# Loops over one ring of rows in place of written-out programs, and two tiny transfers ahead of the others, in a LoRA matrix product on one core

## The chip, the cores and the metric

The kernel runs on one core of a Trainium2 chip. The core has five engines with programs of their own: PE (TensorE, matrix products), DVE (VectorE), ACT (ScalarE), POOL (GpSimd) and SP (SyncE, which here only issues transfers). They meet through semaphores. Transfers between the device's memory and the core's SBUF are issued by SP or ACT and carried by 16 DMA engines, among which each transfer is divided. The metric is the device time of one execution in microseconds (us); lower is better.

## The reference

```python
def reference(x, W, lora_A, lora_B, lora_E, scale):
    x_flat = x.reshape(-1, in_dim)          # 32768 x 256, float32
    y = x_flat @ W                          # W: 256 x 256
    lora_out = x_flat @ lora_A              # 256 x 16
    lora_out = lora_out * lora_E
    lora_out = lora_out @ lora_B            # 16 x 256
    y = y + scale * lora_out
    return y.reshape(batch, seq_len, out_dim)
```

x has 16 x 2048 rows of 256 values, 33.55 MB; the output is as large. Both pass through the core once.

## The kernel before

The rank-16 part is folded into the weights first: weff = W + scale * A diag(E) B, so that each row of x needs one product with a 256 x 256 matrix. PE transposes lora_A (L194), DVE scales it (L132), PE multiplies it by lora_B (L198), DVE adds W (L138, weff in bf16).

The 32768 rows are cut into nine tiles by PLAN (L10): 16 row groups, seven times 32, and 16 again, where a row group is one row for each of the 128 partitions. A 32-row tile is 4096 KB. Each tile is loaded into one of six buffers xy0 to xy5 (SLOTS) of 32 row groups, in which a partition holds 32 consecutive rows, and the result is written over x in the same buffer and stored from there.

SP issues all of the large transfers, in an order that is written out by hand: W (L104), the loads of tiles 0 to 5 (LEAD, L102), and then for each tile a wait until ACT has reported it ready (s_rdy) and its store (L109). After the store of tile 2 come the loads of tiles 6, 7 and 8 (AFTER); each waits until the store that frees its buffer has landed (s_out). All of these use one queue, SP's, so they are carried in this order. ACT issues the three small loads of lora_A, lora_B and lora_E on its own queue (L158 to L160).

The computing runs in 64 steps of four row groups (Q = 4). In a step DVE casts 128 x 1024 values of x to bf16 (xb, L146); PE transposes them in eight blocks into PSUM (ps_xt, L176); DVE copies the transposed blocks to SBUF (xt, L155); PE multiplies them by weff in eight matmuls into PSUM (ps_y, L184); ACT copies the result into the x buffer (L163). xb, xt, ps_xt and ps_y exist twice and alternate. After the last step of a tile, ACT drains and raises s_rdy (L165).

The programs of DVE and ACT are written out: 64 steps one after the other, with waits on rising counts (s_t, s_p). Only PE's program is a loop, of 31 turns with two steps each (L202); there a wait takes its count back down (take, L169). DVE casts one step ahead, and PE transposes one step ahead: the order on PE is transposes of step k + 1, products of step k. DVE itself waits for each tile's load (s_in).

POOL makes the identity matrix for the transposes (L118, L120) and has nothing else to do.

Of the kernel before, what the change touches and what calls it, by code (L numbers as in the profile page):

```python
# [6 lines left out]

PLAN = [16] + [32] * 7 + [16]  # L10

ROWS, SLOTS = 32, 6

LEAD = 6
AFTER = {2: [6, 7, 8]}

Q = 4


@with_exitstack  # L20
def kernel(
    ctx: ExitStack,
    tc: tile.TileContext,
    x: bass.AP,
    W: bass.AP,
    lora_A: bass.AP,
    lora_B: bass.AP,
    lora_E: bass.AP,
    scale: bass.AP,
    out: bass.AP,  # L30
):
    nc = tc.nc
    P = 128
    FP32 = mybir.dt.float32
    BF16 = mybir.dt.bfloat16

    x_flat = x.flatten_outer_dims()
    out_flat = out.flatten_outer_dims()
    N, K = x_flat.shape
    M = out_flat.shape[1]  # L40
    R = lora_B.shape[0]
    KC = K // P
    CHUNKS = len(PLAN)
    assert K == M and sum(PLAN) * P == N and all(b % Q == 0 for b in PLAN)

    def sbuf(name, shape, dt):
        return ctx.enter_context(nc.sbuf_tensor(name, shape, dt))

    def psum(name, shape, dt):
        return ctx.enter_context(nc.psum_tensor(name, shape, dt))  # L50

    xy = [sbuf(f"xy{s}", [P, ROWS, K], FP32) for s in range(SLOTS)]
    xb = [sbuf(f"xb{s}", [P, Q, K], BF16) for s in range(2)]
    xt = [sbuf(f"xt{s}", [P, Q, KC, P], BF16) for s in range(2)]
    w_sb = sbuf("w_sb", [P, KC, M], FP32)
    a_sb = sbuf("a_sb", [P, KC, R], FP32)
    b_sb = sbuf("b_sb", [R, M], FP32)
    e_sb = sbuf("e_sb", [R, 1], FP32)
    b_bf = sbuf("b_bf", [R, M], BF16)
    ate = sbuf("ate", [R, KC, P], BF16)  # L60
    weff = sbuf("weff", [P, KC, M], BF16)
    ident = sbuf("ident", [P, P], FP32)
    ident_bf = sbuf("ident_bf", [P, P], BF16)

    ps_xt = [psum(f"ps_xt{s}", [P, Q, KC, P], BF16) for s in range(2)]
    ps_y = [psum(f"ps_y{s}", [P, Q, M], FP32) for s in range(2)]
    ps_at = psum("ps_at", [P, KC, P], FP32)
    ps_aeb = psum("ps_aeb", [P, KC, M], FP32)

    sem = tc.alloc_semaphore  # L70
    s_w, s_a, s_b, s_e = sem("s_w"), sem("s_a"), sem("s_b"), sem("s_e")
    s_in = [sem(f"s_in{i}") for i in range(CHUNKS)]

    again = CHUNKS - SLOTS
    s_out = [sem(f"s_out{i}") for i in range(again + 1)]
    s_id = sem("s_id")
    s_lora = sem("s_lora")
    s_lpe = sem("s_lpe")
    s_xb = sem("s_xb")
    s_t = sem("s_t")  # L80
    s_xt = sem("s_xt")
    s_p = sem("s_p")
    s_y = sem("s_y")
    s_rdy = sem("s_rdy")

    starts = [sum(PLAN[:i]) * P for i in range(CHUNKS)]

    def rows_of(flat, i):
        b, r0 = PLAN[i], starts[i]
        return flat[r0:r0 + b * P, :].rearrange("(p b) k -> p b k", b=b)  # L90


    steps = [(i, r) for i, b in enumerate(PLAN) for r in range(0, b, Q)]
    n = len(steps)
    assert n % 2 == 0

    with tc.tile_critical(sync_engine=mybir.EngineType.SP, no_gpsimd_drain=True):  # L97
        sp, pe, dve, act, pool = nc.sync, nc.tensor, nc.vector, nc.scalar, nc.gpsimd


        def load(i):
            sp.dma_start(out=xy[i % SLOTS][:, :PLAN[i], :], in_=rows_of(x_flat, i)).then_inc(s_in[i], 16)  # L102

        sp.dma_start(out=w_sb[:], in_=W.rearrange("(c p) m -> p c m", p=P)).then_inc(s_w, 16)  # L104
        for i in range(LEAD):
            load(i)
        for i in range(CHUNKS):
            sp.wait_ge(s_rdy, i + 1)
            sp.dma_start(out=rows_of(out_flat, i), in_=xy[i % SLOTS][:, :PLAN[i], :]).then_inc(s_out[min(i, again)], 16)  # L109
            for later in AFTER.get(i, []):  # L110
                if later >= SLOTS:
                    sp.wait_ge(s_out[later - SLOTS], 16)
                load(later)
        for i in range(len(s_out) - 1):
            sp.wait_ge(s_out[i], 16)


        pool.memset(ident[:], 0.0).then_inc(s_id, 1)  # L118
        pool.wait_ge(s_id, 1)
        pool.affine_select(  # L120
            out=ident[:], in_=ident[:], compare_op=mybir.AluOpType.not_equal, fill=1.0,
            base=0, pattern=[[-1, P]], channel_multiplier=1,
        ).then_inc(s_id, 1)


        dve.wait_ge(s_id, 2)
        dve.tensor_copy(out=ident_bf[:], in_=ident[:]).then_inc(s_lora, 1)  # L127
        dve.wait_ge(s_b, 16)
        dve.tensor_copy(out=b_bf[:], in_=b_sb[:]).then_inc(s_lora, 1)  # L129
        dve.wait_ge(s_e, 16)  # L130
        dve.wait_ge(s_lpe, 1)
        dve.tensor_scalar(  # L132
            out=ate[:], in0=ps_at[:R, :, :], scalar1=e_sb[:], scalar2=float(scale),
            op0=mybir.AluOpType.mult, op1=mybir.AluOpType.mult,
        ).then_inc(s_lora, 1)
        dve.wait_ge(s_w, 16)
        dve.wait_ge(s_lpe, 2)
        dve.tensor_add(out=weff[:], in0=w_sb[:], in1=ps_aeb[:]).then_inc(s_lora, 1)  # L138

        def round_step(k):  # L140
            i, r = steps[k]
            if r == 0:
                dve.wait_ge(s_in[i], 16)
            if k >= 2:
                dve.wait_ge(s_t, k - 1)
            dve.tensor_copy(out=xb[k % 2][:], in_=xy[i % SLOTS][:, r:r + Q, :]).then_inc(s_xb, 1)  # L146

        round_step(0)
        for k in range(n):
            if k + 1 < n:  # L150
                round_step(k + 1)
            dve.wait_ge(s_t, k + 1)
            if k >= 2:
                dve.wait_ge(s_p, k - 1)
            dve.tensor_copy(out=xt[k % 2][:], in_=ps_xt[k % 2][:]).then_inc(s_xt, 1)  # L155


        act.dma_start(out=a_sb[:], in_=lora_A.rearrange("(c p) r -> p c r", p=P)).then_inc(s_a, 16)  # L158
        act.dma_start(out=b_sb[:], in_=lora_B).then_inc(s_b, 16)
        act.dma_start(out=e_sb[:], in_=lora_E[:, None]).then_inc(s_e, 16)  # L160
        for k, (i, r) in enumerate(steps):
            act.wait_ge(s_p, k + 1)
            act.copy(out=xy[i % SLOTS][:, r:r + Q, :], in_=ps_y[k % 2][:]).then_inc(s_y, 1)  # L163
            if r + Q == PLAN[i]:
                act.drain().then_inc(s_rdy, 1)  # L165

        def take(s):  # L169
            pe.wait_ge(s, 1).then_inc(s, -1)  # L170

        def transposes(k):
            take(s_xb)
            for j in range(Q):
                for c in range(KC):
                    t = pe.transpose(ps_xt[k % 2][:, j, c, :], xb[k % 2][:, j, c * P:(c + 1) * P], ident_bf[:])  # L176
            t.then_inc(s_t, 1)

        def products(k):
            take(s_xt)  # L180
            take(s_y)
            for j in range(Q):
                for c in range(KC):
                    m = pe.matmul(  # L184
                        ps_y[k % 2][:, j, :], xt[k % 2][:, j, c, :], weff[:, c, :],
                        start=(c == 0), stop=(c == KC - 1),
                    )
            m.then_inc(s_p, 1)

        pe.sem_inc(s_y, 2)  # L190
        pe.wait_ge(s_a, 16)
        pe.wait_ge(s_id, 2)
        for c in range(KC):
            t = pe.transpose(ps_at[:R, c, :], a_sb[:, c, :], ident[:])  # L194
        t.then_inc(s_lpe, 1)
        pe.wait_ge(s_lora, 3)
        for c in range(KC):
            m = pe.matmul(ps_aeb[:, c, :], ate[:, c, :], b_bf[:], start=True, stop=True)  # L198
        m.then_inc(s_lpe, 1)
        transposes(0)  # L200
        pe.wait_ge(s_lora, 4)
        with pe.Fori(0, n // 2 - 1):  # L202
            transposes(1)
            products(0)
            transposes(0)
            products(1)
        transposes(1)
        products(0)
        products(1)


    with tc.tile_critical(sync_engine=mybir.EngineType.SP, no_gpsimd_drain=True):
        nc.sync.wait_ge(s_out[again], 16 * (CHUNKS - again))
# [34 lines left out]
```

## Time and profile before

| what | value |
|---|---|
| median of 3 runs | 165.41 us (165.13, 165.41, 165.42) |
| the profiled execution | 165.19 us |
| its span, first to last instruction | 163.4 us |
| moved in the span | 67.43 MB, mean 413 GB/s |
| busy: PE, DVE, ACT | 90.8, 84.1, 66.1 us |
| casts of x on DVE (L146) | 64 of 683 ns |
| copies of transposed blocks on DVE (L155) | 64 of 691 ns |
| copies of the result on ACT (L163) | 64 of 1013 ns |
| DMA packets; those of the instruction queue | 3203; 3 |
| SP's waits for ACT's reports (L109) | 77.6 us, 7 times |
| SP's waits for stores before a load (L102) | 38.5 us, 3 times |
| SP's wait for the last store | 36.2 us |

How to read it: the span is the profiled execution from its first to its last instruction; the execution's own time has some 1.8 us around it. A row of slices shows the span in 40 equal parts of 4.085 us; each digit is the busy share in tenths. A table of windows gives, for each stretch, the busy time of PE, its weight loads, DVE, ACT and POOL with the number of instructions, then the granted TensorE clock, the DMA engines' share, and GB/s, where a packet counts in the window in which it starts; so a short window can show more than the engines can carry. Beside these views the trace records each DMA packet with its start, duration, size and queue. Of one queue and one DMA engine the packets follow each other closely, so the packets of one engine can be put in a row by letting each begin where the one before ended; the records don't name the engine.

### The profile page before, as it was taken

How to read it: one execution, taken by the hardware profiler on the slowest of the kernel's cores; microseconds unless marked ns; L12 is line 12 of the kernel's file. 1: busy time of each engine (PE TensorE's matmuls, PEld its weight loads, DVE VectorE, ACT ScalarE, POOL GpSimd, SP SyncE). 2: the span in 40 equal slices, each digit the busy share in tenths (PEclk: the TensorE clock that was granted, in tenths of full speed). 3: DMA queues.
4: the chain of work that ended last, by engine and by line, in shares of the span. 5: the costliest groups of instructions: out<-in, count | busy, mean ns of one | idle time of the engine just before them, and what ended most of it. 6: DMA issues, size and time to landing. Idle time of an engine off the chain costs nothing. (4 is left out here: it accounts for less than half of the span.)

```text
span 163.4 us, 2684 instructions
## 1 busy us (share of the span) xinstructions
PE 90.8 (56%) x1028; PEld 81.6 (50%) x1028; DVE 84.1 (51%) x132; ACT 66.1 (40%) x65; POOL 0.7 (0%) x6
## 2 busy tenths in 40 slices
PE   0169499999999999990000099999992000000000
PEld 0047389999999999980000089999981000000000
DVE  0165299999999999950000169999970000000000
ACT  3002447777777777772000026777774000000000
POOL 1000000000000000000000000000000000000000
PEclk9999999999999999999555559999999755555555
DMA  4999999899999999999999998999999999999990
GB/s 133 421 433 489 393 449 449 385 473 425 403 481 393 385 409 481 393 457 425 433 433 425 441 441 383 465 437 425 425 435 433 441 409 465 417 425 441 409 409 32
DMA packets 3203, 67.43 MB, mean 413 GB/s; under 512 B 624, under 2 KB 896, under 8 KB 896
## 3 DMA queue, kind: packets, MB, share of 16 engines
q1 hardware_dynamic: 2864, 67.37, 96.4%
q10 hardware_dynamic: 336, 0.03, 0.3%
q14 instruction: 3, 0.02, 0.0%
HBM read 33.85 MB, written 33.55 MB: 412 GB/s over the span
## 5 line engine op out<-in xcount | busy, mean ns | idle before, releaser
L163 ACT COPY xy<-ps_y 128x1024 f32<-128x1024 f32 x64 | 64.8, 1013 | 56.2 <-PE ps_y L184 56.2
L184 PE MATMUL ps_y<-weff,xt 128*128 128x256 bf16 x512 | 68.6, 278 | 0.5 <-PEq L170 0.3
L146 DVE CAST xb<-xy 128x1024 bf16<-128x1024 f32 x64 | 43.6, 683 | 24.9 <-DMA xy<-in_x_dram 24.9
L176 PE MATMUL ps_xt<-ident_bf,xb 128*128 128x128 bf16 x512 | 40.9, 226 | 24.7 <-PEq L170 24.7
L184 PEld LDWEIGHTS ps_y<-weff,xt 128*128 128x128 bf16 x512 | 48.4, 100 | 6.4 <-issue 1.1
L176 PEld LDWEIGHTS ps_xt<-ident_bf,xb 128*128 128x128 bf16 x512 | 35.5, 102 | 27.3 <-issue 25.7
L155 DVE COPY xt<-ps_xt 128x1024 bf16<-128x1024 bf16 x64 | 44.2, 691 | 5.4 <-PE ps_xt L176 3.7
L194 PE MATMUL ps_at<-ident,a_sb 128*16 128x128 f32 x2 | 0.6, 402 | 4.1 <-DMA a_sb<-in_lora_A_dram 4.1
L198 PE MATMUL ps_aeb<-b_bf,ate 16*128 16x256 bf16 x2 | 0.6, 404 | 3.6 <-DVE ate L132 3.6
L129 DVE CAST b_bf<-b_sb 16x256 bf16<-16x256 f32 x1 | 0.3, 280 | 3.9 <-DMA b_sb<-in_lora_B_dram 3.9
L163 ACT ACT_TABLE_LOAD x1 | 1.3, 1283 | 2.5 <-issue 2.5
L198 PEld LDWEIGHTS ps_aeb<-b_bf,ate 16*128 16x128 bf16 x2 | 0.1, 106 | 4.1 <-DVE ate L132 4.1
L194 PEld LDWEIGHTS ps_at<-ident,a_sb 128*16 128x16 f32 x2 | 0.1, 94 | 4.1 <-DMA a_sb<-in_lora_A_dram 4.1
L132 DVE TENSOR_SCALAR ate<-ps_at,e_sb 16x256 bf16<-16x256 f32 x1 | 0.5, 472 | 1.6 <-DMA e_sb<-in_lora_E_dram 1.6
L127 DVE CAST ident_bf<-ident 128x128 bf16<-128x128 f32 x1 | 0.2, 227 | 1.7 <-POOL ident L120 1.7
L138 DVE TENSOR_TENSOR weff<-w_sb,ps_aeb 128x512 bf16<-128x512 f32 x1 | 0.7, 687 | 0.8 <-PE ps_aeb L198 0.8
L120 POOL TENSOR_SCALAR_AFFINE_SELECT ident<-ident 128x128 f32<-128x128 f32 x1 | 0.3, 293 | 0.2 <-POOL ident L118 0.2
L118 POOL MEMSET ident<- 128x128 f32 x1 | 0.2, 204 | 0.5 <-SPq L97 0.5
L229 POOL MEMSET const-bfloat16-1.0<- 128x1 bf16 x1 | 0.1, 101 | 0.0
L229 POOL MEMSET const-uint8-127<- 128x1 uint8 x1 | 0.1, 101 | 0.0
L229 POOL MEMSET const-float32-0.0<- 128x1 f32 x1 | 0.1, 98 | 0.2 <-issue 0.2
L229 POOL MEMSET const-float32-1.0<- 128x1 f32 x1 | 0.1, 98 | 0.0
## 6 DMA issues: line engine op xcount, KB each, us to landing
xy<-in_x_dram SPq DMA_DIRECT2D x7, 4096.0 KB, 29.1
out_dram<-xy SPq DMA_DIRECT2D x7, 4096.0 KB, 39.5
xy<-in_x_dram SPq DMA_DIRECT2D x2, 2048.0 KB, 16.3
out_dram<-xy SPq DMA_DIRECT2D x2, 2048.0 KB, 39.3
w_sb<-in_W_dram SPq DMA_DIRECT2D x1, 256.0 KB, 2.9
a_sb<-in_lora_A_dram ACTq DMA_DIRECT2D x1, 16.0 KB, 3.1
b_sb<-in_lora_B_dram ACTq DMA_DIRECT2D x1, 16.0 KB, 4.4
e_sb<-in_lora_E_dram ACTq DMA_DIRECT2D x1, 0.1 KB, 5.7
```

The costliest lines, as they stand in the source:

```text
L120: pool.affine_select(out=ident[:], in_=ident[:], compare_op=mybir.AluOpType.not_equal, fill=1.0, base=0, pattern=[[-1, P]], channel_multip ...
L129: dve.tensor_copy(out=b_bf[:], in_=b_sb[:]).then_inc(s_lora, 1)
L132: dve.tensor_scalar(out=ate[:], in0=ps_at[:R, :, :], scalar1=e_sb[:], scalar2=float(scale), op0=mybir.AluOpType.mult, op1=mybir.AluOpType. ...
L138: dve.tensor_add(out=weff[:], in0=w_sb[:], in1=ps_aeb[:]).then_inc(s_lora, 1)
L146: dve.tensor_copy(out=xb[k % 2][:], in_=xy[i % SLOTS][:, r:r + Q, :]).then_inc(s_xb, 1)
L155: dve.tensor_copy(out=xt[k % 2][:], in_=ps_xt[k % 2][:]).then_inc(s_xt, 1)
L163: act.copy(out=xy[i % SLOTS][:, r:r + Q, :], in_=ps_y[k % 2][:]).then_inc(s_y, 1)
L176: t = pe.transpose(ps_xt[k % 2][:, j, c, :], xb[k % 2][:, j, c * P:(c + 1) * P], ident_bf[:])
L184: m = pe.matmul(ps_y[k % 2][:, j, :], xt[k % 2][:, j, c, :], weff[:, c, :], start=(c == 0), stop=(c == KC - 1),)
L194: t = pe.transpose(ps_at[:R, c, :], a_sb[:, c, :], ident[:])
L198: m = pe.matmul(ps_aeb[:, c, :], ate[:, c, :], b_bf[:], start=True, stop=True)
L229: nc = _bacc.Bacc("TRN2", target_bir_lowering=False, num_devices=1)
```

## The change

The nine tiles become eight of 32 row groups, and the six buffers one ring of 192 row groups (the same memory). Tile i lies at its starting row modulo 192; tiles 6 and 7 reuse the rows of tiles 0 and 1. The two late loads are issued after the store of tile 1.

DVE's and ACT's programs become loops: a turn is eight row groups, two steps. There are two loops one after the other, of 24 turns (the ring once) and of 8 turns, and the address in the ring comes from the loop's register. DVE's order in a turn is cast, cast, copy, copy; PE's is transposes, transposes, products, products, in one loop of 32 turns. All waits take their semaphore back down. ACT drains and reports after every turn, and SP waits for a number of turns. POOL waits for each tile's load and adds a tile's number of turns to a semaphore (s_ld) that DVE's loop takes from.

Ahead of its three small loads, ACT issues two tiny transfers of 16 pieces of 64 bytes each, one piece for each DMA engine: one reads 16 places of the first tile of x into a spare tile, first_x; the other writes values of lora_A to 16 places of the output, which the store of tile 0 overwrites later. SP waits for both before its first store.

```diff
-PLAN = [16] + [32] * 7 + [16]
-ROWS, SLOTS = 32, 6
+PLAN = [32] * 8
+RING = 192
 LEAD = 6
-AFTER = {2: [6, 7, 8]}
+AFTER = {1: [6, 7]}
 Q = 4
+TURN = 2 * Q
...
-    xy = [sbuf(f"xy{s}", [P, ROWS, K], FP32) for s in range(SLOTS)]
+    xy = sbuf("xy", [P, RING, K], FP32)
+    xy_turns = xy[:].rearrange("p (t k q) d -> p t k (q d)", k=2, q=Q)
...
+    first_x = sbuf("first_x", [16, R], FP32)
...
+    def corners(flat):
+        return flat[:PLAN[0] * P, :].rearrange("(e b) k -> e b k", e=16)[:, 0, :R]
+    def ring_of(i):
+        r = starts[i] % RING
+        return xy[:, r:r + PLAN[i], :]
+    passes = [RING, sum(PLAN) - RING]
+    turns = sum(PLAN) // TURN
...
         for i in range(LEAD):
             load(i)
+        sp.wait_ge(s_first, 32)
         for i in range(CHUNKS):
-            sp.wait_ge(s_rdy, i + 1)
+            sp.wait_ge(s_rdy, (starts[i] + PLAN[i]) // TURN)
...
             for later in AFTER.get(i, []):
-                if later >= SLOTS:
-                    sp.wait_ge(s_out[later - SLOTS], 16)
+                sp.wait_ge(s_out[owner[later]], 16)
                 load(later)
...
+        for i in range(CHUNKS):
+            pool.wait_ge(s_in[i], 16).then_inc(s_ld, PLAN[i] // TURN)
...
-        round_step(0)
-        for k in range(n):
-            if k + 1 < n:
-                round_step(k + 1)
-            dve.wait_ge(s_t, k + 1)
-            if k >= 2:
-                dve.wait_ge(s_p, k - 1)
-            dve.tensor_copy(out=xt[k % 2][:], in_=ps_xt[k % 2][:]).then_inc(s_xt, 1)
+        for rows in passes:
+            with dve.Fori(0, rows // TURN) as turn:
+                take(dve, s_ld)
+                for k in range(2):
+                    dve.tensor_copy(out=xb[k][:], in_=xy_turns[:, bass.ds(turn, 1), k, :]).then_inc(s_xb, 1)
+                for k in range(2):
+                    take(dve, s_t)
+                    dve.tensor_copy(out=xt[k][:], in_=ps_xt[k][:]).then_inc(s_xt, 1)
...
+        act.dma_start(out=first_x[:], in_=corners(x_flat)).then_inc(s_first, 16)
+        act.dma_start(out=corners(out_flat), in_=lora_A[:16, :]).then_inc(s_first, 16)
         act.dma_start(out=a_sb[:], in_=lora_A.rearrange("(c p) r -> p c r", p=P)).then_inc(s_a, 16)
...
-        for k, (i, r) in enumerate(steps):
-            act.wait_ge(s_p, k + 1)
-            act.copy(out=xy[i % SLOTS][:, r:r + Q, :], in_=ps_y[k % 2][:]).then_inc(s_y, 1)
-            if r + Q == PLAN[i]:
+        for rows in passes:
+            with act.Fori(0, rows // TURN) as turn:
+                for k in range(2):
+                    take(act, s_p)
+                    act.copy(out=xy_turns[:, bass.ds(turn, 1), k, :], in_=ps_y[k][:]).then_inc(s_y, 1)
                 act.drain().then_inc(s_rdy, 1)
...
-        transposes(0)
         pe.wait_ge(s_lora, 4)
-        with pe.Fori(0, n // 2 - 1):
+        with pe.Fori(0, turns):
+            transposes(0)
             transposes(1)
             products(0)
-            transposes(0)
             products(1)
-        transposes(1)
-        products(0)
-        products(1)
```

## Prediction

> **What bounds the kernel now.** I read the page's slices first, then the table of DMA queues, then short windows at both ends, and last one step of the compute loop.
>
> ```profile
> PE   0169499999999999990000099999992000000000
> DVE  0165299999999999950000169999970000000000
> DMA  4999999899999999999999998999999999999990
> ...
> q1 hardware_dynamic: 2864, 67.37, 96.4%
> q10 hardware_dynamic: 336, 0.03, 0.3%
> q14 instruction: 3, 0.02, 0.0%
> ```
>
> The DMA row is full from the second slice to the last but one, while PE and DVE pause for some 20 us in the middle and are done at 125 us. SP's queue alone fills 96.4% of sixteen engines' time: the transfers bound the kernel, and computing costs nothing while every store is issued before its turn. So the time is: start, 67 MB at a fixed pace, and the end. In the trace's packet records a 32 KB packet takes 1.213 us, and a 32-row transfer is 8 of them on each of 16 engines, one every 9.68 us; a 16-row transfer takes 4.87 us. The end is the place to look at:
>
> ```profile
> 158.00:159.00 1.00, 0.00 (x0) 0.00 (x0) 0.00 (x0) 0.00 (x0) 0.00 (x0) 0.50 0.99 426
> 159.00:160.00 1.00, 0.00 (x0) 0.00 (x0) 0.00 (x0) 0.00 (x0) 0.00 (x0) 0.50 0.39 164
> 160.00:161.00 1.00, 0.00 (x0) 0.00 (x0) 0.00 (x0) 0.00 (x0) 0.00 (x0) 0.50 0.08 33
> 161.00:162.00 1.00, 0.00 (x0) 0.00 (x0) 0.00 (x0) 0.00 (x0) 0.00 (x0) 0.50 0.08 33
> 162.00:163.40 1.40, 0.00 (x0) 0.00 (x0) 0.00 (x0) 0.00 (x0) 0.00 (x0) 0.50 0.00 0
> ```
>
> The last two numbers are DMA share and GB/s. At 159 us the share falls from 0.99 to 0.39, then to 0.08 for two microseconds: a few engines are still at work. By the packet records the last store ends at 159.15 us on the first engine, at 159.5 on the median one, and at 161.65 and 161.73 on two stragglers, which I call B and A. SP's last wait ends with them; 1.67 us later the span ends, and the run's 165.19 us lie 1.79 us over its span of 163.4. So the sum goes by the later straggler: 161.73 + 1.67 + 1.79 = 165.19. Any gain must come from A and B both.
>
> I followed their packets (each starts where the one before on its engine ended). A lost 0.95 us at 41.7 and 0.66 us at 119.0, each just after one of the three 8 KB instruction packets of queue 14 (41.4, 101.6, 118.7), and 0.88 us at the first store. B met no instruction packet. It lost 0.43 us in its first x packet, 1.01 us at the first store, and 2.4 us in small portions: about 100 ns on each 32 KB store packet, at 57.8 to 71.8 and 105.2 to 121.5 us. These are the stretches in which a store runs and DVE works; loads beside DVE, and stores after it, are not slowed. I don't know the cause. The first store is seen in windows, too (436 GB/s is the mean of 30 to 54 us):
>
> ```profile
> 54.00:56.00 2.00, 2.00 (x25) 1.84 (x23) 1.94 (x5) 1.63 (x2) 0.00 (x0) 1.00 0.78 279
> 56.00:58.00 2.00, 2.00 (x28) 1.88 (x27) 1.95 (x4) 1.45 (x2) 0.00 (x0) 1.00 0.97 369
> ```
>
> Here the last load runs out and the first write to out begins. The median engine ends that load 0.49 us late; no later change between load and store costs the median engine anything.
>
> **The change, part by part, for B and A.**
>
> The plan: 14 transfers of 9.68 and 4 of 4.87 (155.0 us) become 16 of 9.68 (154.9): -0.1 us, bounds -0.2 and 0.
>
> The loops on DVE and ACT: their written-out programs should need no instruction packet in the run. A gains 1.6 us (bounds 0 and 1.6), B nothing. By itself that is worth 161.73 - 161.65 = 0.08 us: B is as late.
>
> The tiny write into out: if the loss at the first store is a one-time cost of an engine's first write there, and it is paid at 3 us, B gains up to 1.01 us and A 0.88. But SP's own W and x packets are in the engines from 2.0 us on, and the ACT queue's first packets come at 2.7, so it may be paid again in part. Bounds -1.0 and 0 for B; I take the middle, -0.5.
>
> The tiny read of x: x's first packets lose 0.43 us on B, 0.64 in the median, gaps included. The tiny one comes perhaps half a microsecond ahead and puts 64 more packets of nearly nothing into the engines. Bounds -0.4 and +0.3; I take -0.1.
>
> Two more issues on ACT (0.49 and 0.53 us for those there now) push lora_A, lora_B and lora_E back by 1.0 us and weff from 9.65 to 10.7. That is hidden: with 32 rows the first x tile lands at 3.3 + 0.64 + 9.68 = 13.6, and as now about 0.8 us goes by until DVE begins, 14.4. SP's new wait on the two tiny ones stands before the first store, behind all six first loads; they land at about 5 us, the store is ready at 28, and even 60 would do. POOL's relay of loads to DVE adds a semaphore step per tile, under 0.1 us, on idle engines.
>
> The compute loop decides whether stores stay in time. One step now is bound by PE and DVE together:
>
> ```profile
> 101.14 0.68 DVE L146 CAST xb<-xy 128x1024 bf16<-128x1024 f32 x1
> 101.21 0.61 PE L176 MATMUL ps_xt<-ident_bf,xb 128*128 128x128 bf16 x8
> 101.41 1.01 ACT L163 COPY xy<-ps_y 128x1024 f32<-128x1024 f32 x1 [0.31 <-PE ps_y L184]
> 101.60 0.81 PEld L184 LDWEIGHTS ps_y<-weff,xt 128*128 128x128 bf16 x8
> 101.65 1.04 PE L184 MATMUL ps_y<-weff,xt 128*128 128x256 bf16 x8
> 101.85 0.69 DVE L155 COPY xt<-ps_xt 128x1024 bf16<-128x1024 bf16 x1
> 102.42 0.54 PEld L176 LDWEIGHTS ps_xt<-ident_bf,xb 128*128 128x128 bf16 x8
> ...
> 102.53 0.61 PE L176 MATMUL ps_xt<-ident_bf,xb 128*128 128x128 bf16 x8
> ```
>
> A step is 1.32 us: 0.44 from transposes to products, 0.88 from products to the next transposes. The new turn of two steps no longer transposes ahead. From its first transposes: 0.64 to DVE's copy (101.21 to 101.85), 0.69 for it, 0.30 to the products (a copy ends at 122.34, products start at 122.64), 2 x 0.88 for both: 3.39 us in place of 2.64. DVE's next two casts fit beneath the products with some 0.6 us over for its loop. PE's own loop, the nearest row, has 208 ns for a compare and branch and 36 for its sum: 0.24 per turn, hidden ahead. Bounds for a turn: 3.39, and 4.4 if DVE's loop with its computed addresses costs 1 us past that cover. I take 3.4. ACT needs 2 x 1.01 and a drain per turn and isn't the bound; the drain's 1042 ns are the copy it waits for.
>
> So compute ends at 14.4 + 2 (PE's first groups of products take up to 1.9 us in place of 1.04) + 32 x 3.4 + 1 = 126 us. New order of transfers: x to 62, two stores to 81.4, loads to 100.8, then stores every 9.68, the last from 149.2. The one after a slot's release is issued while another 9.7 us transfer runs, so the engines never wait for SP. The last store must be issued by 147: that breaks at 14.4 + 2 + 32P + 1 = 147, a turn of 4.05 us. Cover: 21 us.
>
> But a longer stretch of DVE work beside stores lengthens B's loss. Now about 23 steps lie beside stores for 2.4 us, 0.105 each. Then: 14 turns before 62, 5.7 beside the two stores, 5.7 beside loads, 6.6 beside stores again: 24.6 steps, 2.6 us: +0.2. Bounds: -2.4, if the loss is not tied to DVE and stays away, and +1.2, if every one of 36 store packets up to 124 us pays 100 ns.
>
> The Trainium skill speaks against loops: "Runtime: NRT & Kernel Launch", section "Instruction fetch mechanics", says that a taken branch to a page out of the current window forces a fetch before anything goes on. The rows above don't agree for PE: its loop branches back 31 times here, and queue 14 has three packets in the whole run. Were it so for DVE or ACT, every turn would have an instruction packet in it; by the rows the term is 0, by the page 32 stalls of a length that no run here shows; at 1 us each the sum would be that of rival 3.
>
> Sum for B: 161.65 - 0.1 - 0.5 - 0.1 + 0.2 = 161.15. For A: 161.73 - 0.1 - 1.6 - 0.5 - 0.1 = 159.4, below B. The end moves by 161.15 - 161.73 = -0.6: 165.19 - 0.6 = 164.6. The median of the runs shown is 165.41, 0.22 over the profiled one; as they spread by 0.29 I add nothing, and with the leaning of B's bounds to the lower side I say 164.5, 0.55% less than the median.
>
> **Rivals.** (1) B's small losses go with the written-out programs, or the tracing alone makes them: then ordinary engines end it. The latest of these now ends at 160.0; less 0.1 and 0.5, 159.4, so 162.9 (bounds 162.7 to 163.6). For: loads don't suffer, so it isn't plain contention; against: it comes and goes with DVE's work, which stays.
>
> (2) The change of transfers does nothing: first costs are merely paid at 3 us, and B decides: 161.65 - 0.1 + 0.2, no change, 165.2. For: the engines are already busy when the tiny ones arrive.
>
> (3) Slower by a late last store: DVE's loop, its only uncovered part, makes a turn longer than 4.05 us. At 4.4 compute ends at 158; the last store is issued 11 us too late, and the time is some 176. For: no row shows a computed address on DVE; against: PE's 0.24 against a slack of 0.6 + 0.65.
>
> (4) Slower by B: +1.2 and no gain at the first store: 161.65 - 0.1 + 1.2 = 162.75, time 166.2. B is later than now as soon as its added loss beside stores is more than the 0.1 of the plan and what the first store gives back.
>
> **Chances.** Forecast (164.0 to 164.9) 0.42, (1) 0.22, (2) 0.16, (3) 0.07, (4) 0.13. A measurement of this kernel tells 0.2%, 0.33 us, from no change. Faster: 0.42 + 0.22 + a little of (2), 0.66; within: 0.15; slower: 0.19. The range holds all but (3) and the outer ends of (1) and (4): 162.9 to 166.0; the likeliest case's own is 164.0 to 164.9.
>
> **What would show it.** No instruction packets in the span; a turn near 3.4 us and compute done near 126; bandwidth not dipping at the first store (62 us), but near 3 us; DMA share with a shorter tail than 2.2 us. Wrong would be: an idle slice in DMA's row after 100 us (rival 3), or one engine as late as before with the dip gone (rival 4).

## The result: slower by 2.5%, and the profile after

The changed kernel takes 169.61 us (median of 4 runs, 169.05 to 169.80) against 165.32 us for the kernel before in the same comparison; the ratio is 1.0255, with a 95% interval of 1.0228 to 1.0283. The forecast was 164.5 us, with a range that ended at 166.0.

These are lines of the page of the changed kernel: its slices (40 parts of 4.2 us), its DMA queues, and groups of instructions.

```profile
PE   0000001168777777677777776677777778885000
DVE  0000000275765566666665566666655777753000
ACT  0000000007878888888788888888788654566000
...
DMA  5999999999999999999998999999999995890894
...
q1 hardware_dynamic: 2576, 67.37, 93.8%
q10 hardware_dynamic: 400, 0.04, 0.2%
...
L186 ACT ACT_TABLE_LOAD x24 | 30.8, 1283 | 51.4 <-ACTq L146 51.4
...
L212 PE MATMUL ps_at<-ident,a_sb 128*16 128x128 f32 x2 | 0.6, 402 | 27.0 <-DMA a_sb<-in_lora_A_dram 27.0
...
a_sb<-in_lora_A_dram ACTq DMA_DIRECT2D x1, 16.0 KB, 24.9
b_sb<-in_lora_B_dram ACTq DMA_DIRECT2D x1, 16.0 KB, 27.0
e_sb<-in_lora_E_dram ACTq DMA_DIRECT2D x1, 0.1 KB, 28.9
```

Three things are new. The compute engines do next to nothing until slice 7: PE waits 27.0 us for lora_A, which lands 24.9 us after its issue, where it took 3.1. ACT loads its table of functions 24 times, 1.28 us each, where it did so once. And the DMA row, full until slice 33, has two holes near its end. Queue 14 has no line any more: no instruction packet falls into the span. The lines of the kernel before for the landing and the table load:

```profile
a_sb<-in_lora_A_dram ACTq DMA_DIRECT2D x1, 16.0 KB, 3.1
...
L163 ACT ACT_TABLE_LOAD x1 | 1.3, 1283 | 2.5 <-issue 2.5
```

The late first product, in order of time (start, duration, engine, line, operation):

```profile
26.99 0.60 PE L212 MATMUL ps_at<-ident,a_sb 128*16 128x128 f32 x2 [26.99 <-DMA a_sb<-in_lora_A_dram]
29.67 0.28 DVE L152 CAST b_bf<-b_sb 16x256 bf16<-16x256 f32 x1 [27.74 <-DMA b_sb<-in_lora_B_dram]
32.13 0.47 DVE L155 TENSOR_SCALAR ate<-ps_at,e_sb 16x256 bf16<-16x256 f32 x1 [2.18 <-DMA e_sb<-in_lora_E_dram]
...
33.37 0.69 DVE L161 TENSOR_TENSOR weff<-w_sb,ps_aeb 128x512 bf16<-128x512 f32 x1 [0.77 <-PE ps_aeb L216]
33.97 1.29 DVE L169 CAST xb<-xy 128x1024 bf16 x2
```

All three small loads are waited for, one after the other, and DVE makes its first cast of x at 33.97 us. The first tile had been there since about 14.

Two turns of the loop in the changed kernel, the parts of ACT and PE:

```profile
61.61 1.28 ACT L186 ACT_TABLE_LOAD   x1 [0.54 <-ACTq L146]
...
62.90 1.93 ACT L186 COPY xy<-ps_y 128x1024 f32 x2
64.03 1.70 PEld L202 LDWEIGHTS ps_y<-weff,xt 128*128 128x128 bf16 x16 [1.06 <-issue]
...
65.37 1.28 ACT L186 ACT_TABLE_LOAD   x1 [0.54 <-ACTq L146]
...
66.66 1.93 ACT L186 COPY xy<-ps_y 128x1024 f32 x2
67.79 1.70 PEld L202 LDWEIGHTS ps_y<-weff,xt 128*128 128x128 bf16 x16 [1.06 <-issue]
```

A turn is 66.66 - 62.90 = 3.76 us, and ACT fills it: table load 1.28, two copies 1.93, and 0.54 in which it drains and waits for PE's first products. These in turn wait until ACT has copied the last ones out of ps_y, so the table load lies in the circle. In the last 8 turns, those of the second loop, no table is loaded and a turn is 3.49 us (149.12 - 145.63):

```profile
145.63 1.28 DVE L169 CAST xb<-xy 128x1024 bf16 x2
149.12 1.28 DVE L169 CAST xb<-xy 128x1024 bf16 x2
```

The holes, in windows (the last two numbers are DMA share and GB/s):

```profile
140.00:142.00 2.00, 1.31 (x21) 1.14 (x19) 1.07 (x2) 1.58 (x2) 0.00 (x0) 1.00 0.08 33
142.00:144.00 2.00, 2.00 (x23) 1.81 (x23) 1.42 (x3) 0.85 (x1) 0.00 (x0) 1.00 1.20 508
...
152.00:154.00 2.00, 1.61 (x15) 1.47 (x16) 0.69 (x2) 0.44 (x2) 0.00 (x0) 1.00 0.08 33
154.00:156.00 2.00, 0.30 (x3) 0.02 (x1) 0.00 (x0) 1.55 (x2) 0.00 (x0) 1.00 0.00 0
156.00:158.00 2.00, 0.00 (x0) 0.00 (x0) 0.00 (x0) 0.00 (x0) 0.00 (x0) 1.00 1.23 524
```

ACT finishes the last tile at 155.6, SP issues its store then, and the packets begin at 156.5; most engines had ended the store before it at 152.3 and wait 4.2 us, after some 2.6 us of waiting for the one before. The share of 0.08 in the first hole is one engine, the slow one, which is still behind.

### The profile page after: what moved, and what is told of

Its sections match the earlier page's. It is cut to its first block, busy times and chain, and to the rows that moved or that the text cites. A ratio compares the mean times of both kernels' runs of the same rounds, so it can differ in the third digit from the quotient of the medians.

```text
span 168.0 us, 3155 instructions
## 1 busy us (share of the span) xinstructions
PE 93.8 (56%) x1028; PEld 78.8 (47%) x1028; DVE 81.5 (49%) x132; ACT 92.5 (55%) x88; POOL 0.7 (0%) x6
## 5 line engine op out<-in xcount | busy, mean ns | idle before, releaser
L202 PE MATMUL ps_y<-weff,xt 128*128 128x256 bf16 x512 | 63.1, 275 | 26.9 <-PEq L146 26.9
L186 ACT COPY xy<-ps_y 128x1024 f32 x64 | 61.7, 1015 | 11.7 <-ACTq L146 11.5
L202 PEld LDWEIGHTS ps_y<-weff,xt 128*128 128x128 bf16 x512 | 46.6, 98 | 40.0 <-issue 31.6
L172 DVE COPY xt<-ps_xt 128x1024 bf16<-128x1024 bf16 x64 | 41.3, 686 | 38.8 <-DVEq L146 38.8
L169 DVE CAST xb<-xy 128x1024 bf16 x64 | 41.1, 685 | 0.0
L194 PE MATMUL ps_xt<-ident_bf,xb 128*128 128x128 bf16 x512 | 34.6, 222 | 1.5 <-PEq L146 1.5
L194 PEld LDWEIGHTS ps_xt<-ident_bf,xb 128*128 128x128 bf16 x512 | 31.9, 99 | 2.7 <-issue 2.0
## 6 DMA issues: line engine op xcount, KB each, us to landing
a_sb<-in_lora_A_dram ACTq DMA_DIRECT2D x1, 16.0 KB, 24.9
```

What stands on the lines that cost most here:

```text
L169: dve.tensor_copy(out=xb[k][:], in_=xy_turns[:, bass.ds(turn, 1), k, :]).then_inc(s_xb, 1)
L172: dve.tensor_copy(out=xt[k][:], in_=ps_xt[k][:]).then_inc(s_xt, 1)
L186: act.copy(out=xy_turns[:, bass.ds(turn, 1), k, :], in_=ps_y[k][:]).then_inc(s_y, 1)
L194: t = pe.transpose(ps_xt[k][:, j, c, :], xb[k][:, j, c * P:(c + 1) * P], ident_bf[:])
L202: m = pe.matmul(ps_y[k][:, j, :], xt[k][:, j, c, :], weff[:, c, :], start=(c == 0), stop=(c == KC - 1),)
```

## The experiments

One rival was that the table loads in ACT's loop alone make the stores late. The theory was that they would not, without the late start: 14.3 + 2 + 24 x 3.76 + 8 x 3.49 = 135 us, well before 147. Ratios are against the kernel before, from the same comparison; the changed kernel was compared on its own, so its median stands beside the others' only to some 0.3 us.

| kernel | median us | ratio, 95% interval | DVE's first cast of x |
|---|---|---|---|
| the changed kernel | 169.61 | 1.0255, 1.0228 to 1.0283 | 33.97 |
| loops, no tiny transfers | 167.18 | 1.0095, 1.0079 to 1.0112 | 14.29 |
| small loads first | 167.15 | 1.0087, 1.0068 to 1.0105 | 14.56 |
| table loaded ahead | 168.26 | 1.0154, 1.0125 to 1.0182 | 33.04 |
| tiny transfers only | 166.39 | 1.0043, 1.0026 to 1.0060 | 31.88 |
| late small loads, no tiny transfers | 168.37 | 1.0157, 1.0129 to 1.0185 | 31.94 |
| loops, no tiny transfers, table ahead | 166.82 | 1.0070, 1.0047 to 1.0094 | 14.08 |
| the same, pipelined | 166.47 | 1.0044, 1.0025 to 1.0063 | 14.12 |

**Loops without the tiny transfers.**

```diff
-        sp.wait_ge(s_first, 32)
...
-        act.dma_start(out=first_x[:], in_=corners(x_flat)).then_inc(s_first, 16)
-        act.dma_start(out=corners(out_flat), in_=lora_A[:16, :]).then_inc(s_first, 16)
```

> The changed kernel without the two tiny transfers and without the wait on them; the loops, the ring and the table load inside ACT's loop stay. Theory (late start): the small loads are issued at 0.9 us again, ahead of x's 32 KB packets, and land in 3 to 6 us; DVE casts from about 14.4 us, compute ends at 14.4 + 2 + 24 x 3.76 + 8 x 3.49 = 135 us, and no store is late: no idle slice of the DMA engines. What is left is the one slow engine: some 44 store packets beside DVE's work at 0.1 us, 4.4 us behind the median engine's 159.3, so 159.3 + 4.4 + 1.67 + 1.79 = 167.1. If that slow engine is made by the tracing alone, the timed runs lie near 163.5 and only the profiled one near 167. Rival (ACT's table loads in the loop make the stores late by themselves): idle slices before the last two stores stay, 169 or more.

167.18 us. The DMA row of this page, with lora_A's landing:

```profile
DMA  6998998989989899999899999999999999999940
...
a_sb<-in_lora_A_dram ACTq DMA_DIRECT2D x1, 16.0 KB, 3.3
```

The holes are gone though ACT's table loads are still in the loop. So the table loads alone don't make a store late. What is left over the kernel before, 1%, is a longer tail of one engine: by the packet records the last store ends at 159.28 us on the median engine and at 163.57 on the slow one. In windows (a share of 0.08 over 1 us is one 32 KB packet, of one engine):

```profile
161.00:162.00 1.00, 0.00 (x0) 0.00 (x0) 0.00 (x0) 0.00 (x0) 0.00 (x0) 0.50 0.08 33
162.00:163.00 1.00, 0.00 (x0) 0.00 (x0) 0.00 (x0) 0.00 (x0) 0.00 (x0) 0.50 0.08 33
163.00:164.00 1.00, 0.00 (x0) 0.00 (x0) 0.00 (x0) 0.00 (x0) 0.00 (x0) 0.50 0.00 0
```

Each run has one such engine. The records don't name it, so that it is the same one in every run is not shown.

**Small loads first.**

```diff
-        act.dma_start(out=first_x[:], in_=corners(x_flat)).then_inc(s_first, 16)
-        act.dma_start(out=corners(out_flat), in_=lora_A[:16, :]).then_inc(s_first, 16)
         act.dma_start(out=a_sb[:], in_=lora_A.rearrange("(c p) r -> p c r", p=P)).then_inc(s_a, 16)
...
         act.dma_start(out=e_sb[:], in_=lora_E[:, None]).then_inc(s_e, 16)
+        act.dma_start(out=first_x[:], in_=corners(x_flat)).then_inc(s_first, 16)
+        act.dma_start(out=corners(out_flat), in_=lora_A[:16, :]).then_inc(s_first, 16)
```

> The changed kernel with ACT's three small loads issued ahead of the two tiny transfers. Theory (late start): the small loads land within 3 to 6 us, compute ends near 135 us, no store is late; against the kernel without the tiny transfers 0 to -0.8 us, if the first store costs less, so 166.3 to 167.1. Rival (the tiny write into out itself blocks ACT's queue or the engines): the first x packets or the small loads still land late, and the time stays near 169.6.

167.15 us, at the upper end of what was expected and not to be told from the loops without any tiny transfers: behind the small loads they do neither harm nor good that can be seen. What did harm is their place.

**Table loaded ahead.**

```diff
+        act.wait_ge(s_id, 2)
+        act.copy(out=warm[:], in_=ident[:, :1])
         for rows in passes:
             with act.Fori(0, rows // TURN) as turn:
```

> The changed kernel with one small copy on ACT (a column of the identity into a spare tile) ahead of its loops, so that the activation table is loaded once and no longer in every turn of the first loop; the tiny transfers stay first. Theory (late start is the larger part): the turn falls from 3.76 to 3.49 us, compute begins at 34 us as in the changed kernel and ends at 34 + 2 + 32 x 3.49 = 148 us; the last store is just in time, the 6.7 us of idle DMA engines go, and the slow engine, 5 us behind, ends it: 167.5 to 168.2. Rival (the table loads are the whole cause): 165 or less. Rival (the table loads don't matter, for PE or DVE sets the turn): 169.6 as before.

168.26 us, a little above the expected 168.2.

```profile
DMA  5999989999899999999989999998999999998910
...
L184 ACT ACT_TABLE_LOAD x1 | 1.3, 1283 | 3.7 <-issue 3.7
```

One table load is left in the run, the holes are gone, and the slow engine, 5.6 us behind the median one, ends the kernel. So the table loads cost where the late start had used up the cover: 1.35 us of medians, a part of which is that DVE began 0.9 us sooner here.

**Tiny transfers only**, on the kernel before: the same two issues and SP's wait, nothing else.

```diff
         for i in range(LEAD):
             load(i)
+        sp.wait_ge(s_first, 32)
...
+        act.dma_start(out=first_x[:], in_=corners(x_flat)).then_inc(s_first, 16)
+        act.dma_start(out=corners(out_flat), in_=lora_A[:16, :]).then_inc(s_first, 16)
         act.dma_start(out=a_sb[:], in_=lora_A.rearrange("(c p) r -> p c r", p=P)).then_inc(s_a, 16)
```

> The kernel before with the two tiny transfers first and SP's wait on them; its written-out programs stay. Theory (late start, covered by a step of 1.32 us): the small loads land some 25 us late, DVE begins at 34 us in place of 9.6, compute of the first six tiles ends near 92 us and of all near 125, no store is late. More stores run beside DVE's work, 30 in place of 24 packets' worth, +0.6 us; a cheaper first store, 0 to -0.5: 165.3 to 166.0. Rival (the tiny transfers cost or gain by themselves): under 164.6, or over 167.

166.39 us, above the stated 165.3 to 166.0; against the 165.65 of the kernel before in this comparison it is 0.74 us, where 0.6 less whatever the first store gives back was expected. Computing starts 22 us late here, too, but a step is 1.32 us and no store comes late.

**Late small loads, no tiny transfers.** ACT waits for the bf16 identity, an event at 2 us that has nothing to do with transfers:

```diff
+        act.wait_ge(s_lora, 1)
         act.dma_start(out=a_sb[:], in_=lora_A.rearrange("(c p) r -> p c r", p=P)).then_inc(s_a, 16)
```

> The changed kernel without the tiny transfers, but ACT waits until DVE has made the bf16 identity (about 2.0 us) before it issues the three small loads, so that these go out as late as behind the two tiny transfers. Theory (the loss is the place in the engines' queues: behind the first x packets each 64-byte packet of lora_A waits for a 32 KB packet): lora_A lands about 24 us after its issue, DVE's first cast of x is at 33 to 34 us, and the time is that of the changed kernel, 169 to 170. Rival (the tiny transfers themselves, the write into out above all, held the small loads up): they land within 3 to 8 us, and the time stays at 167.2.

```profile
DMA  5999989989999898999989899999989996980992
...
a_sb<-in_lora_A_dram ACTq DMA_DIRECT2D x1, 16.0 KB, 22.8
b_sb<-in_lora_B_dram ACTq DMA_DIRECT2D x1, 16.0 KB, 25.2
e_sb<-in_lora_E_dram ACTq DMA_DIRECT2D x1, 0.1 KB, 27.1
```

The landings say that it is the moment of issue, not the tiny transfers: one microsecond later, and 16 KB need 22.8 us in place of 3.3. The holes near the end are back. The time, 168.37, is under the expected 169 to 170: DVE starts at 31.94, 2 us sooner than in the changed kernel, which has two transfers more in that queue.

**Loops without the tiny transfers, table ahead.** The edit of "table loaded ahead" on the loops without tiny transfers.

> The loops without the tiny transfers and with the activation table loaded ahead of them: against the loops without the tiny transfers, this is the price of the table loads where compute starts in time. The turn is 3.49 in place of 3.76 us, so compute ends at 128 in place of 135; no store is late in either. If the table loads cost only by making stores late: 166.9 to 167.3, no difference to 167.2 that can be told (the slow engine passes the same stores beside nearly as many instructions). If the length of the compute loop counts by itself: 165.5 to 166.

166.82 us, between the two expected ranges; the interval overlaps that of the kernel with table loads in the loop, so the table loads' price where compute is in time can't be told from nothing. Beside "table loaded ahead", where no store was late either, it shows that a covered late start isn't free: 168.26 against 166.82 us. There more of the stores run beside computing, and the slow engine ends at 165.06 in place of 163.58.

**Pipelined**: on the last kernel, casts and transposes go one step ahead again, across turns.

```diff
-                take(dve, s_ld)
-                for k in range(2):
-                    dve.tensor_copy(out=xb[k][:], in_=xy_turns[:, bass.ds(turn, 1), k, :]).then_inc(s_xb, 1)
-                for k in range(2):
-                    take(dve, s_t)
-                    dve.tensor_copy(out=xt[k][:], in_=ps_xt[k][:]).then_inc(s_xt, 1)
+                cast(1, bass.ds(turn, 1))
+                moved(0)
+                cast(0, bass.ds(turn + 1, 1))
+                moved(1)
...
-        with pe.Fori(0, turns):
-            transposes(0)
+        with pe.Fori(0, turns - 1):
             transposes(1)
             products(0)
+            transposes(0)
             products(1)
```

> The loops without the tiny transfers, with the table loaded ahead, and with the order of the kernel before: DVE casts and PE transposes one step ahead across the turns. Theory: no instruction packet in the run, the step is 1.32 us again, compute beside stores is as long as in the kernel before, and the slow engine ends near 161.5, as there; the straggler that the instruction packets made is gone. So 164.9 to 165.5 against 165.5, no difference that can be told. If the time goes by the length of the compute loop alone it must be 1.7 us or more below the unpipelined loops' 167.2.

166.47 us: slower than the kernel before and not below 165.5. The step is 1.32 us again and no instruction packet is in the run, but the slow engine ends at 163.63, 2 us later than in the kernel before. Beside full steps it lost 99 to 146 ns a packet, 118 in the mean, in place of 100, and 1.1 us in one packet at 100.8 us, where the last load turns into a store. The one packet is the larger part. In the kernel before the slow engine has no such loss there; in the eight kernels with loops it has one each, of 0.58 to 1.23 us at 100.1 to 100.8 us. These kernels have the new plan too, and what makes that loss was not followed. The small losses led to the next question.

**What slows that engine? Fewer instructions on PE.**

```diff
             for j in range(Q):
-                for c in range(KC):
-                    m = pe.matmul(
-                        ps_y[k % 2][:, j, :], xt[k % 2][:, j, c, :], weff[:, c, :],
-                        start=(c == 0), stop=(c == KC - 1),
-                    )
+                m = pe.matmul(
+                    ps_y[k % 2][:, j, :], xt[k % 2][:, j, 0, :], weff[:, 0, :],
+                    start=True, stop=True,
+                )
```

> The kernel before with half of every product left out (the contraction's second 128 rows are not added, so 4 matmuls a step in place of 8); transposes, DVE's and ACT's work stay. It asks what slows the one engine's store packets. If it goes by the number of PE's instructions: 24 with weight loads in place of 32 per step, so about 75 ns a packet in place of 100 beside a full step. If it goes by DVE's work, whose share stays: 100 ns. The time moves by under 0.6 us in either case.

Its one run took 165.60 us, within the 0.6 us that either theory allowed. The packets beside full steps lose 80 to 108 ns, 88 in the mean, not 75 and not 100. The step had become shorter, too (1.20 us), so I counted per microsecond. In the table, "instructions" are all that the trace records on all engines, waits and branches included, and "loss" is what the slow engine's 32 KB store packets lose, both in the same stretch:

| kernel, stretch (us) | instructions per us | loss, ns per us | ns per instruction |
|---|---|---|---|
| loops, no tiny, 65 to 81 | 25.7 | 65.2 | 2.54 |
| fewer on PE, 107.5 to 116.8 | 27.0 | 71.3 | 2.64 |
| before, 107.5 to 118.5 | 30.5 | 79.3 | 2.60 |
| tiny only, 63.5 to 81 | 30.5 | 82.2 | 2.69 |
| pipelined, 105.6 to 117 | 35.1 | 89.9 | 2.56 |

**Instructions that do nothing.** To the kernel before, POOL gets 80 turns of four raises and four waits on a semaphore of its own.

```diff
+        pool.wait_ge(s_in[CHUNKS - 1], 16)
+        with pool.Fori(0, 80):
+            for _ in range(4):
+                pool.sem_inc(s_more, 1)
+                pool.wait_ge(s_more, 1).then_inc(s_more, -1)
```

> The kernel before with idle work added on POOL: once the last tile of x has landed (106 us), 80 turns of eight instructions that raise and lower a semaphore nobody else uses, some 800 instructions with the loop's own, beside the stores; no data, no DVE, no PE. In the ten traces so far the slow engine's store packets lose 2.5 to 2.8 ns for every instruction that any engine is recorded to run meanwhile. If the loss goes by the number of instructions: 800 x 2.6 ns = 2.1 us more on that engine, packets slowed until POOL ends near 150 us, the time 1.9 to 2.2 us above the kernel before. If it comes from DVE's or PE's access to the memories: no change, within 0.3 us.

185.40 us, which says nothing: a turn took 0.92 us, so POOL itself ended the kernel at 183 us. The packets do say something. Where they lost 103 ns they lose 159, and from 127 to 150 us, where PE, DVE and ACT are idle and the kernel before shows no loss, each loses 33 to 61 ns, with POOL's 10.9 instructions per us beside it. The last packet of that engine ends at 163.76, 2.1 us later than before. That it is the expected number is in part luck: some 600 of POOL's instructions lay beside stores, not 800, and each cost about 3.3 ns, not 2.6.

With 38 turns POOL is done in time:

> The same idle work on POOL with 38 turns in place of 80: a turn took 0.92 us in that trace, so POOL runs from 107 to some 142 us and no longer ends the kernel itself. 380 instructions with the loop's own; 380 x 2.6 to 3.3 ns = 1.0 to 1.25 us more on the slow engine, whose last packet moves from 161.7 to near 162.8: the time is 0.9 to 1.3 us over the kernel before. If what slows that engine is DVE's or PE's work alone: no change, within 0.3 us.

166.55 us against 165.71, 1.0054 (1.0033 to 1.0074), some 0.9 us, at the lower end of what was expected and clear of no change. The slow engine ends at 163.01. POOL's waits in this trace (count, ns, first and last start), and then its last windows:

```profile
L129 POOLq EVENT_SEMAPHORE  x152: 17/17/17, 108.9 to 143.4; - x152
```

```profile
161.00:162.00 1.00, 0.00 (x0) 0.00 (x0) 0.00 (x0) 0.00 (x0) 0.00 (x0) 0.50 0.15 66
162.00:163.00 1.00, 0.00 (x0) 0.00 (x0) 0.00 (x0) 0.00 (x0) 0.00 (x0) 0.50 0.04 16
```

POOL is idle from 143 us on, and the tail still reaches past 162 us, where the kernel before has 161.7. So instructions that touch no data slow this engine, where DVE's and PE's use of memory can't be the reason. That the losses beside computing have the same cause is argued from their nearly equal price, 2.5 to 2.8 ns per instruction in every kernel; POOL's instructions cost about a quarter more.

**Leave the slow engine out of the last store**, to turn that into a gain, on the loops with the table ahead:

```diff
+            else:
+                sp.dma_start(out=o[:, :EVEN, :], in_=y[:, :EVEN, :]).then_inc(done, 16)
+                sp.dma_start(out=o[:120, EVEN:, :], in_=y[:120, EVEN:, :]).then_inc(done, 16)
+                sp.dma_start(out=o[120:, EVEN:, :], in_=y[120:, EVEN:, :]).then_inc(done, 16)
```

> The loops without the tiny transfers and with the table loaded ahead, and the last store cut in three: the first 16 rows of every partition as before, of the other 16 rows partitions 0 to 119 in one transfer, which 15 engines share, and partitions 120 to 127 in another, which 8 engines share. If the slow engine is the one that these two leave out, it moves 128 KB less, 4.8 us, and its lag of some 4 us is gone; eight engines move 16 KB more, 0.6 us, so the last packet is near 160.2 and the time near 163.6. If the slow engine is among the others: 167 to 167.8.

169.99 us, worse than either expectation. By the packet records the engine that was left out ended at 155.1, ordinary until then, and the slow one at 166.99: the wrong engine was spared. And from 155 us on the 16 KB packets of the last stores took longer on most engines, 1.21 us in the median from 156 to 158 us in place of 0.61. In windows:

```profile
156.00:158.00 2.00, 0.00 (x0) 0.00 (x0) 0.00 (x0) 0.00 (x0) 0.00 (x0) 0.50 0.75 180
158.00:160.00 2.00, 0.00 (x0) 0.00 (x0) 0.00 (x0) 0.00 (x0) 0.00 (x0) 0.50 0.98 287
160.00:162.00 2.00, 0.00 (x0) 0.00 (x0) 0.00 (x0) 0.00 (x0) 0.00 (x0) 0.50 0.56 147
```

For its busy share this moves 0.56 to 0.68 of the bytes that full windows of the kernel before move (426 GB/s at 0.99). Why a store cut so is slow wasn't followed. No version tried beats the kernel before.

## Why the prediction was wrong, step by step

**The step that failed** is "Two more issues on ACT (0.49 and 0.53 us for those there now) push lora_A, lora_B and lora_E back by 1.0 us and weff from 9.65 to 10.7. That is hidden". The issue of lora_A did come 1.15 us later, but I took the landing to move with the issue. In the kernel before, lora_A's 256 pieces of 64 bytes ran from 2.7 to 3.6 us, in a gap that closes: x's first packets begin at 3.15. A microsecond later each piece stands beside a 32 KB packet of x on its engine, 16 pieces of lora_A per engine, and each of them waits for one: by the packet records the pieces follow each other every 1.22 us, as x's packets do, and 16 x 1.22 = 19.5 us. DVE began at 33.97 and not at 14.4. The row was there to see: I had read W's packets ending at 3.3 us and lora_A's on queue 10 starting at 2.7, and compared neither with the new time. The same fact was in my text for the tiny transfers ("SP's own W and x packets are in the engines from 2.0 us on") and wasn't applied to what stands behind them. The late-small-loads kernel shows the cause alone; against the small-loads-first kernel, which differs in the order of the issues alone, the changed one lost 2.46 us of medians by it (1.7% by the two ratios, some 2.8 us). The rest of the 2.55%, 0.9%, is the slow engine's, below.

**A second miss**: ACT's "2 x 1.01 and a drain per turn and isn't the bound". ACT has one table load in the kernel before, 1.28 us at 2.5 us, inside the line of the copy. In a loop whose body is the first place that needs the table, the load is in the body: 24 x 1.28 us. The turn became ACT's, 3.76 us. By itself that changed nothing that can be told; on top of the late start it made the last two stores late, and that ended the changed kernel: all engines end the last store at 166.2 to 166.4 us, the slow one with them.

**Rival 3** named the right end, a last store past 147 us, with the wrong cause: DVE's loop. DVE's computed addresses show no cost: in the pipelined kernel, which has them, a step is 1.32 us as before. The turn worked out as 3.39 was 3.49 without table loads. From the measured start and turns the rule gives 34 + 2 + 24 x 3.76 + 8 x 3.49 = 154; the last store was issued at 155.6.

**The slow engine**: I gave B "+0.2", with a bound of +1.2. It measured +1.9 (163.57 in the loops without tiny transfers, 161.65 before). About 0.9 us of this are the small losses, 3.3 us in place of 2.4. I had priced them by steps beside stores; they go with instructions, and the loops run more of them (3152 in place of 2684) and run them for longer beside stores. Another 0.86 us is one packet at 100.1 us, where the second load turns into a store, a term that the sum didn't have; its cause is open. Together this is most of the 1% by which the loops stay slower.

**The tiny write into out**, "-0.5": not shown. I compare the end of the last of the six first loads with that of the one before on the median engine, less 9.69: 0.34, 0.46 and 0.59 us in the three loop kernels with the tiny write, 0.10, 0.55, 0.75, 0.97 and 1.07 in the five without it, 0.49 in the kernel before and 0.04 in that kernel with the tiny write. It varies with something else; what, stays open. The tiny read's -0.1 can't be seen either.

**Right were**: the transfers as what bounds the kernel before; and no instruction packets with loops, so that straggler A is gone. In the kernels whose programs are all loops no instruction packet falls into the span. I set these rows against the Trainium skill, "Runtime: NRT & Kernel Launch", section "Instruction fetch mechanics"; but that rule is for a branch to a page out of the current window, and no run here shows such a branch, so it is neither shown nor refuted. The plan's -0.1 us can't be told: the median engine ends at 159.28 in one loop kernel and at 159.74 in another, 159.48 before.

## What to carry to other kernels

A small transfer that everything waits for must be issued before the large ones reach the DMA engines: look up when the first large packet starts, and treat that as a deadline, not as a delay that adds up. When written-out code becomes a loop, ask what its first pass did once, such as loading a function table, and do it ahead of the loop. And cover is one sum: the late start and the longer turn each left every store in time, both together did not. Even a covered delay had a price here, 0.7 us (tiny transfers only) to 1.4 us (table ahead), as it moved computing beside the stores.

## What the runs showed of the hardware that I had not expected

Small pieces beside large packets: 16 KB landed 3.1 to 3.3 us after an issue at 0.9 us, and 22.8 to 24.9 us after one at 2.0 us. The Trainium skill has the rule, "DMA: Bandwidth & Descriptors", section "Queues, rings and completion order": an engine goes round robin over its queues, a packet at a time. The traces agree, with one piece of 64 bytes for one packet of 32 KB, 1.22 us each.

One DMA engine of the sixteen pays for instructions: its store packets beside them lose 2.5 to 2.8 ns for each instruction recorded on any engine meanwhile (24.6 to 35.1 per us in ten traces), 3.1 to 3.3 ns where POOL's semaphore instructions run alone; its loads beside computing show no such loss. Every run here has its span and clock recorded, and whether it is this recording that goes through that engine, so that an unrecorded run would not have the tail, no run here can tell.
